# Placeholders in the job lists of a two-layer encoder: key steps one dense chunk further on, first inverse two further on in layer 2

## The chip, the core and the metric

The kernel runs on one core of a Trainium2 chip. The metric is device time in microseconds, lower is better. A matrix product runs on TensorE (PE), elementwise work on VectorE (DVE), ScalarE (ACT) and GpSimd (POOL); transfers are issued from the queues of SyncE (SP), ACT and POOL and carried by 16 DMA engines.

## The reference, cut to what matters

A trunk of two layers over 1024 tokens and 16 learned ones, width 1024, in float32. Each layer norms its input, projects it, and runs two groups side by side: a chunked gated delta rule in both directions (four heads of 128) and a gated short convolution. Their outputs go through one projection and a residual, then a SwiGLU block.

```
h = h + hybrid_mixer(rmsnorm(h), w_in, ...)       # per layer
h = h + swiglu(rmsnorm(h), w_gate_up, w_down)

# in hybrid_mixer
q, k, v = split(silu(conv3(qkv)));  q = l2norm(q);  k = l2norm(k)
# in the delta rule, per chunk, head and direction
M = strict_lower(beta * k @ k.T * decay);  A = M + I
u = solve(A, beta * v);  w = solve(A, beta * k * exp(G))
attn = q @ k.T * decay;  q_dec = q * exp(G)
# then a scan over the chunks: S, o
y_sc = sc_b * conv3(sc_c * sc_h)
out = concat(norm(o) * silu(z), y_sc) @ w_out
```

## The kernel before, in words

The sequence is worked on as nine chunks: one of 16 tokens and eight of 128. Features lie on the 128 partitions and tokens along the free axis (1040 columns).

**Dense work.** `dense` (L141 to L170) forms a product of a weight tile with eight tiles of the input, for one stretch of columns (a chunk of the dense work) at a time. Float32 exactness comes from splitting both factors into a high and a low part, so one dense chunk is 8 x 3 = 24 products (L156, L157, L158) into a bank `pacc`. A full row tile has three dense chunks, 348 or 346 columns wide; the z tiles of the last layer and some others have two, 512 wide. An eviction follows on DVE (`to_row`, L295). Weights come in as `raw` (L128, SP's queue) and are split on ACT (L129) and on POOL or DVE (L130).

**Job lists.** After each dense chunk `dense` takes one entry off each of `jobs`, `jobs2` and `jobs3` and calls it; `None` is a placeholder that lets one dense chunk go by. So the small steps of the delta rule are strewn among the large products. This fixes the order in which the program is written; the order on each engine is then decided by a scheduler, which places instructions by priority and by when its own timeline has their operands ready. `low` (L685) gives a step the priority of the dense products around it.

**Order within a layer.** Four key tiles, then four query tiles, then four value tiles, then the gated convolution and the z tiles.

- After the fourth key tile the key lengths are ready: `normalise` (L408) takes the root on ACT (L412) and the reciprocal on DVE (L413), sends them out and back as a row on all partitions by POOL's queue (L415, L418), and scales the keys head by head on DVE (L419).
- `k_out` (L421), one call a chunk: four transposes of the keys on PE (L427) into the single bank `pa`, a copy on ACT (L429) into a tile `kt`, a store by ACT's queue (L430).
- `chunk_p` (L448), one call a chunk: products of the keys with themselves (L456) into a bank `pb`; for each direction a load of decays `gd` by ACT's queue (L459), an addition on DVE (L460), the exponential on ACT (L462), a store to `dtd` by ACT's queue (L463) and the product into `P` on DVE (L465).
- `sub_start` (L511) copies the diagonal blocks of 32 x 32 on ACT (L521) and transposes them on DVE (L523). `substitute` (L525) solves these blocks by 31 steps of two instructions on DVE (L533, L535).
- `invert` (L537) builds the inverse of the 128 x 128 blocks from them in seven steps, each an entry of `jobs3`. It begins with two transposes on DVE (L544, L545) and four copies on ACT (L547). The first step multiplies on PE (L560, 128 products of 32 x 32 into `pf`, for the second direction into `pb`) and copies on ACT (L563); the second likewise (L568, L571), the third (L578, L579 to L582), the fourth (L589, L590) and the fifth (L594, L595).
- `chunk_a` (L483), one call a chunk: products of keys with queries (L489) into one of two banks `pb`; for each direction a load `eg` by ACT's queue (L493), a product on DVE (L494), a store by SP's queue (L496), a load `dt` of what `chunk_p` stored (L498, ACT's queue), a product on DVE with the bank (L499), a store by SP's queue (L501).
- `v_store` (L693), three calls a value tile: transposes on PE into `pa` (L695, L706), a copy on DVE into `vm` (L699) or on ACT (L707), a store (L702, L708).
- `z_tile` (L673) and the value tiles apply a Silu on ACT (L678, L720), the key and query tiles too (L632, followed by a square, L633, whose sums over the partitions are formed on PE, L606); `conv` (L306 to L309) is a copy on ACT and two steps on DVE.

The small tiles `eg`, `dt`, `kt`, `vm`, `rows` and a few more share one tag (`ck2`) with five buffers, used in turn. The banks of PSUM are `pacc` (three), `pa` (one), `pf` (two) and `pb` (two).

The steps of the first inverse enter `jobs3` as the fourth value tile begins (L716); those of the second inverse follow later, among the z tiles.

Of the kernel before, what the change touches and what calls it, by code (L numbers as in the profile page):

```python
# [42 lines left out]
def trunk(ctx: ExitStack, tc: tile.TileContext, xT, w_in, w_ba, w_out, w_gu, w_dn,  # L43
# [8 lines left out]
    def nm(p):  # L52
        cnt[0] += 1
        return f"{p}_{cnt[0]}"

    def big(tag, dt=F32):
        return sb.tile([128, 4, L], dt, tag=tag, name=nm(tag))
# [4 lines left out]
    def t2k(tag):  # L62
        return sb.tile([128, 4, 128], F32, tag="ck2", bufs=5, name=nm(tag))

    def c4k(tag="c"):
        return sb.tile([128, L], F32, tag="c", bufs=2, name=nm(tag))

    def bank(tag):
        return psp.tile([128, 512], F32, tag=tag, bufs={"acc": 3, "a": 1, "f": 2, "b": 2}[tag], name=nm("p" + tag))

    def pa():
        return bank("a")
# [47 lines left out]
    jobs, jobs2, jobs3 = [], [], []  # L120
# [158 lines left out]
    for l in range(DEPTH):  # L279
# [9 lines left out]
        def inproj(i, evac, pool=None, chunks=FULL):  # L289
            ws = pre.pop(i) if i in pre else wload(w_in[l, i], KT)  # L290
            dense(ws, x, chunks, evac, pool)

        def to_row(t):
            def f(ps, n0, n1):
                tt(out=t[:, n0:n1], in0=ps, in1=rstd[:, n0:n1], op=ALU.mult)  # L295
            return f

        def to_row_late(t):
            def f(ps, n0, n1):
                nc.vector.tensor_copy(t[:, n0:n1], ps)  # L300
            return f

        def trow():
            return row(Y[1], F32, 3)
# [27 lines left out]
        def gate_weights():  # L332
            dma(wr, w_ba[l])
            act(out=wb[:, :, 0:16], in_=wr, func=AF.Copy)
            tt(out=wb[:, :, 16:32], in0=wr, in1=wb[:, :, 0:16].bitcast(F32), op=ALU.subtract)
# [85 lines left out]
        def k_out(c):  # L421

            n = 16 if c == 0 else 128
            s0 = 0 if c == 0 else 16 + 128 * (c - 1)
            ps = pa()
            for h in range(H):
                nc.tensor.transpose(ps[0:n, h * 128:(h + 1) * 128], KTt[:, h, s0:s0 + n], ident)  # L427
            kt = t2k("kt")
            act(out=kt[0:n].rearrange("p a b -> p (a b)"), in_=ps[0:n], func=AF.Copy)  # L429
            adma(vkd[c, 0:n, 1, :], kt[0:n].rearrange("p a b -> p (a b)"))  # L430
# [10 lines left out]
        def span(c):  # L441
            return (16, 0) if c == 0 else (128, 16 + 128 * (c - 1))
# [3 lines left out]
        def chunk_p(c):  # L446

            if not Pd:  # L448
                Pd.extend(sb.tile([128, 4 * L], F32, tag=f"P{d}", name=nm("P")) for d in range(2))
                Pv.extend(p[:, 0:4096].rearrange("p (q i) -> p q i", i=128) for p in Pd)  # L450
                p_ = sb.tile([128, 4 * L], F32, tag=Y[0][2], name=nm("ptm"))
                ptm.extend(p_[:, 512 * i:512 * i + 512].rearrange("p (h i) -> p h i", h=4) for i in range(8))
            n, s0 = span(c)
            kk = bank("b").rearrange("p (h i) -> p h i", h=4)
            for h in range(H):
                mm(kk[0:n, h, 0:n], KTt[:, h, s0:s0 + n], KTt[:, h, s0:s0 + n], start=True, stop=True)  # L456
            for d in (dirs0 if c == 0 else (0, 1)):
                gr = ptm[(2 * c + d) % 8]
                adma(gr[0:n, :, 0:n], gd[36 * d + 4 * c:36 * d + 4 * c + 4, 0:n].partition_broadcast(n))  # L459
                tt(out=gr[0:n, :, 0:n], in0=gr[0:n, :, 0:n], in1=off[0:n, d, 0:n].unsqueeze(1).to_broadcast([n, 4, n]), op=ALU.add)  # L460
                for h in range(H):
                    act(out=gr[0:n, h, 0:n], in_=gr[0:n, h, 0:n], func=AF.Exp, scale=-1.0, bias=nGb[0:n, d, c, h:h + 1])  # L462
                adma(dtd[c, d].rearrange("p (h i) -> p h i", h=4)[0:n, :, 0:n], gr[0:n, :, 0:n])  # L463
                dst = P0[d] if c == 0 else Pv[d][:, 4 * c - 4:4 * c, :]
                tt(out=dst, in0=kk[0:n, :, 0:n], in1=gr[0:n, :, 0:n], op=ALU.mult)  # L465
                if c == 0:

                    def meta():
                        mt = t2k("mt").rearrange("p a b -> p (a b)")[0:4].rearrange("p (w a b) -> p w a b", w=2, a=16)
                        Wm, Zm = mt[:, 0], mt[:, 1]  # L470
                        Tm = t2k("mt").rearrange("p a b -> p (a b)")[0:4, 0:256].rearrange("p (a b) -> p a b", a=16)
                        dma(m0d[d, 0].rearrange("h j i -> j h i"), P0[d])
                        dma(Wm, m0d[d, 0])
                        dma(Zm, eye_d[0:4, :, :][:, 0:16, 0:16])
                        for s in (range(15, 0, -1) if d == 0 else range(0, 15)):
                            r0, r1, a0, a1 = (0, s, s, 16) if d == 0 else (s + 1, 16, 0, s + 1)
                            sh = [4, r1 - r0, a1 - a0]
                            ptt(out=Tm[:, r0:r1, a0:a1], in0=Wm[:, r0:r1, s:s + 1].to_broadcast(sh), in1=Zm[:, s:s + 1, a0:a1].to_broadcast(sh), op=ALU.mult)
                            ptt(out=Zm[:, r0:r1, a0:a1], in0=Zm[:, r0:r1, a0:a1], in1=Tm[:, r0:r1, a0:a1], op=ALU.subtract)
                        dma(m0d[d, 1], Zm)  # L480
                        dma(P0[d], m0d[d, 1].rearrange("h j i -> j h i"))

                    meta()  # L483
# [26 lines left out]
        def sub_start():  # L510

            nonlocal Tm
            tmp0.append(big(Y[0][2]))
            Tm = sb.tile([128, 2, 128], F32, tag="off", name=nm("Tm")).rearrange("p a b -> p (a b)")
            v = [tmp0[0][:, i, 0:1024] for i in range(4)]
            for d in range(2):
                W, Xi = (v[0], v[2]) if d == 0 else [c4k("x")[:, 0:1024] for _ in range(2)]
                W, Xi, dg = (t.rearrange("p (a b) -> p a b", a=32) for t in (W, Xi, v[3 - 2 * d]))
                dma(Xi, eye_d)
                for b in range(4):  # L520
                    act(out=dg[B[b]], in_=Pv[d][B[b], :, B[b]], func=AF.Copy)  # L521

                nc.vector.transpose(out=W, in_=dg.rearrange("p q i -> p i q"))  # L523
                subs[d] = W, Xi
# [106 lines left out]
        def lengths(which, q, row_, buf):  # L631
            act(out=row_, in_=row_, func=AF.Silu)  # L632
            act(out=buf, in_=row_, func=AF.Square)  # L633
            jobs.append(lambda: sums(which, q, buf))

        seq = (4, 5, 6, 7, 0, 1, 2, 3)
        for pos, i in enumerate(seq):
            hh = pos % 4
            if pos == 2:
                gate_weights()  # L640
                evp[0] = base - 60000
            lov[0] = pos > 3
            t = trow()
            late = pos < (2, 1)[l]
            inproj(i, to_row_late(t) if late else to_row(t), pfirst if l == 0 and pos == 1 else None)
            if late:
                tt(out=t, in0=t, in1=rstd, op=ALU.mult)
            dst = (QT if i < 4 else KTt)[:, hh, :]
            conv(t, dst, P_CV + 3 * i)
            if i >= 4:  # L650
                lengths("k", hh, dst, t)
            if pos == 2:
                g, negG, nGb, negE, gl, bkd = gates()
            nxt = seq[pos + 1] if pos < 7 else 8
            if nxt not in pre:
                pre[nxt] = wload(w_in[l, nxt], KT)
            if pos == 3:
                jobs.append(None)
                jobs.extend([lambda c=c: k_out(c) for c in range(9)])
                jobs2.extend([None, None] + [lambda c=c: chunk_p(c) for c in range(9)])  # L660

        for hh in range(4):
            lengths("q", hh, QT[:, hh, :], c4k("sq"))
        qs_ = jobs[-4:]
        del jobs[-4:]
        jobs.extend([None, None, None, lambda: [f() for f in qs_]])
        sub_start()
        substitute(0)

# [41 lines left out]
        for i in range(4):  # L711
            t = trow()
            if i == 2:
                jobs2.extend([lambda c=c: chunk_a(c) for c in ca])
            if i == 3:
                jobs3.extend(invert(0))  # L716
            inproj(8 + i, to_row(t))
            v = trow() if i % 2 == 0 else row(Y[1] + "f")
            conv(t, v, P_CV + 3 * (8 + i))
            act(out=v, in_=v, func=AF.Silu)  # L720
            jobs.extend([lambda i=i, v=v, c0=c0: v_store(i, v, c0) for c0 in (0, 1, 5)])
# [157 lines left out]
        for i, (d, s) in enumerate(order):  # L879
            at_prio(base - 17000 + 4000 * (1 - d) + 400 * s)  # L880
            c = s if d == 0 else 8 - s
# [108 lines left out]
        for m in range(KT + 2):  # L990
# [14 lines left out]
            else:  # L1005
                c = pcol(P_N2 + k)
# [496 lines left out]
```

## Time and profile before

| | |
|---|---|
| time, median of 3 runs | 2607.66 us (2607.26 to 2610.53) |
| the profiled execution's own time | 2614.81 us |
| its span, first to last instruction | 2612.7 us |
| mean granted TensorE clock | 0.984 |
| PE busy | 2508.1 us, 96% |
| DVE busy | 1654.4 us, 63% |
| ACT busy | 1045.9 us, 40% |
| POOL busy | 1105.0 us, 42% |
| DMA, mean rate over the span | 137 GB/s |

How to read it: times in the trace count from the first instruction of the span. Layer 1's steps named above lie at about 120 to 300 us, layer 2's at about 1418 to 1610 us. In a row of the timeline the bracket at the end gives how long the engine had been idle and what ended that. A row of the waits has the line that waited, what it waited for, the total, the number of times, and the longest. An instruction on PE is shown with its whole time in the pipeline, so the pace of a row of products is the distance of their starts.

### The profile page before, as it was taken

The page shows a single profiled execution, that of the slowest core. Times are in us where ns is not written, and L with a number is a line of the kernel's source. Part 1 is how long each engine was busy: PE and PEld are TensorE (multiplying, and loading weights), DVE is VectorE, ACT ScalarE, POOL GpSimd, SP SyncE. Part 2 cuts the span into 40 slices and gives each one's busy share as a digit, 9 for nine tenths or more (in the row PEclk, how much of TensorE's full clock was granted, in tenths as well). Part 3 has the DMA queues.
Part 4 walks back from the last instruction along what each step waited for, and adds up shares of the span by engine and source line. Part 5 has one row for each costly group of instructions (what it writes and reads, how often), then busy time and mean ns, then how long its engine had stood idle before and what let it go on. Part 6 is the DMA issues. An engine that isn't in the chain of part 4 may idle for free.

```text
span 2612.7 us, 45153 instructions
## 1 busy us (share of the span) xinstructions
PE 2508.1 (96%) x17442; PEld 2294.1 (88%) x17442; DVE 1654.4 (63%) x2481; ACT 1045.9 (40%) x1933; POOL 1105.0 (42%) x838
## 2 busy tenths in 40 slices
PE   8999999999999999989999989999989999998997
PEld 6989999898899999989999978998967778886876
DVE  4688433648766666667656874236688777668656
ACT  5664322435233333434445633324452333333444
POOL 2141311225666666645321203122367667665552
PEclk9999999999999999989999999999999999999998
DMA  3458264524422222763324581545333222248431
GB/s 126 135 185 268 90 215 148 176 80 125 135 91 99 94 74 74 252 198 111 97 86 136 186 283 63 182 159 197 116 121 129 94 102 85 79 141 273 133 108 65
DMA packets 213571, 360.03 MB, mean 138 GB/s; under 512 B 25268, under 2 KB 87676, under 8 KB 213356
## 3 DMA queue, kind: packets, MB, share of 16 engines
q1 hardware_dynamic: 180684, 310.69, 36.1%
q10 hardware_dynamic: 30496, 42.09, 5.1%
q0 software_dynamic: 2176, 4.36, 0.6%
q8 instruction: 137, 2.24, 0.4%
q14 instruction: 78, 0.64, 0.1%
HBM read 266.60 MB, written 90.46 MB: 137 GB/s over the span
## 4 chain that ended last, share of the span: by engine, by line
PE 54%; DVE 9%; DMA 4%; issue 3%; POOL 2%; ACT 1%; POOLq 0%; ACTq 0%; DVEq 0%; SPq 0%
PE pacc L156 5%; PE pacc L158 5%; PE pacc L157 5%; PE pacc L1060 3%; PE pacc L1062 3%; PE pacc L1061 3%; PE pb L1060 2%; PE pf L1060 2%; PE pb L1062 2%; PE pb L1061 2%; PE pf L1062 2%; PE pf L1061 2%; PE pacc L1400 1%; PE pacc L1402 1%; PE pacc L1401 1%
## 5 line engine op out<-in xcount | busy, mean ns | idle before, releaser
L130 POOL TENSOR_TENSOR wlo<-raw,whi 128x512 fp32r<-128x512 f32 x132 | 177.0, 1342 | 788.3 <-ACT whi L129 639.4
L156 PE MATMUL pacc<-a,whi 128*128 128x346 f32 (+1 forms) x808 | 265.5, 332 | 10.2 <-ACT whi L129 8.3
L158 PE MATMUL pacc<-a,wlo 128*128 128x346 f32 (+1 forms) x808 | 265.1, 330 | 0.4 <-DVE wlo L130 0.4
L156 PE MATMUL pacc<-b,whi 128*128 128x346 f32 (+2 forms) x672 | 234.8, 350 | 0.0
L158 PE MATMUL pacc<-b,wlo 128*128 128x346 f32 (+2 forms) x672 | 233.2, 348 | 0.0
L157 PE MATMUL pacc<-a,whi 128*128 128x346 f32 (+1 forms) x688 | 227.5, 331 | 2.7 <-DVE a L900 2.5
L129 ACT ACTIVATE whi<-raw 128x512 fp32r<-128x512 f32 x168 | 105.3, 629 | 244.6 <-PE pacc L157 169.3
L157 PE MATMUL pacc<-b,whi 128*128 128x346 f32 (+2 forms) x580 | 200.5, 347 | 0.5 <-DVE b L900 0.5
L156 PEld LDWEIGHTS pacc<-a,whi 128*128 128x128 f32 x808 | 154.5, 192 | 14.5 <-ACT whi L129 10.1
L1043 POOL TENSOR_TENSOR wlo<-rw,whi 128x512 fp32r<-128x512 f32 x92 | 134.8, 1467 | 71.7 <-ACT whi L1042 70.0
L158 PEld LDWEIGHTS pacc<-a,wlo 128*128 128x128 f32 x808 | 154.5, 191 | 2.1 <-issue 0.8
L157 PEld LDWEIGHTS pacc<-a,whi 128*128 128x128 f32 x688 | 132.2, 192 | 7.1 <-issue 2.9
L156 PEld LDWEIGHTS pacc<-b,whi 128*128 128x128 f32 x672 | 127.3, 190 | 11.0 <-issue 3.1
L158 PEld LDWEIGHTS pacc<-b,wlo 128*128 128x128 f32 x672 | 127.3, 190 | 9.2 <-issue 0.8
L1043 POOL TENSOR_TENSOR a<-rw,a 128x512 fp32r<-128x512 f32 x64 | 105.6, 1651 | 69.5 <-ACT a L1042 69.3
L1043 POOL TENSOR_TENSOR b<-rw,b 128x512 fp32r<-128x512 f32 x64 | 92.0, 1439 | 82.3 <-ACT b L1042 49.5
L157 PEld LDWEIGHTS pacc<-b,whi 128*128 128x128 f32 x580 | 109.9, 190 | 7.8 <-DVE b L900 1.0
L1042 ACT ACTIVATE whi<-rw 128x512 fp32r<-128x512 f32 x92 | 57.8, 630 | 146.5 <-DVE rw L1270 84.8
L1266 DVE TENSOR_TENSOR rw<-rw,rw 128x512 f32<-128x512 f32 x44 | 67.4, 1532 | 49.9 <-POOL wlo L1043 34.6
L1271 DVE TENSOR_TENSOR rw<-raw,rw 128x512 f32<-128x512 f32 x44 | 97.4, 2214 | 1.2
L1043 POOL TENSOR_TENSOR wlo<-raw,whi 128x512 fp32r<-128x512 f32 x50 | 76.6, 1533 | 36.5 <-ACT whi L1042 27.9
L1042 ACT ACTIVATE b<-rw 128x512 fp32r<-128x512 f32 x64 | 40.2, 630 | 119.8 <-PE pacc L1061 32.3
(970 smaller groups left out, 8420.2 us busy)
## 6 DMA issues: line engine op xcount, KB each, us to landing
raw<-in_w_in SPq DMA_DIRECT2D x112, 256.0 KB
raw<-in_w_gu SPq DMA_DIRECT2D x104, 256.0 KB
rw<-in_w_gu SPq DMA_DIRECT2D x88, 256.0 KB
rec<-aqd SPq DMA_DIRECT2D x62, 256.0 KB
rec<-vkd SPq DMA_DIRECT2D x61, 256.0 KB
rw<-in_w_dn SPq DMA_DIRECT2D x70, 192.0 KB
raw<-in_w_out SPq DMA_DIRECT2D x48, 256.0 KB
b<-ad SPq DMA_DIRECT2D x45, 260.0 KB
```

The lines of the kernel that those rows point to most:

```text
L129: act(out=hi, in_=raw[:, 0:kk, :], func=AF.Copy)
L130: (tt if lov[0] else ptt)(out=lo, in0=raw[:, 0:kk, :], in1=hi.bitcast(F32), op=ALU.subtract)
L156: mm(ps[:, :n], wh, xh[:, n0:n1], start=(k == 0), stop=False)
L157: mm(ps[:, :n], wh, xl[:, n0:n1], start=False, stop=False)
L158: mm(ps[:, :n], wl, xh[:, n0:n1], start=False, stop=(k == K - 1))
L1042: act(out=hi, in_=src, func=AF.Copy)
L1043: ptt(out=lo, in0=src, in1=hi.bitcast(F32), op=ALU.subtract)
L1060: mm(ps[:, :CW], w[0][:, k, :], th[:, cs], start=first and k == 0, stop=False, skip_group_check=True)
L1061: mm(ps[:, :CW], w[0][:, k, :], tl[:, cs], start=False, stop=False, skip_group_check=True)
L1062: mm(ps[:, :CW], w[1][:, k, :], th[:, cs], start=False, stop=stop and k == nk - 1, skip_group_check=True)
L1266: tt(out=s1t, in0=A21, in1=A22, op=ALU.add)
L1271: tt(out=A21, in0=A11, in1=A21, op=ALU.subtract)
```

## The change

Two edits in the order in which steps are put into the job lists; nothing that is computed changes.

1. After the fourth key tile, in both layers: two placeholders instead of one stand ahead of the nine `k_out` in `jobs`, and three instead of two ahead of the nine `chunk_p` in `jobs2`. An `assert` states that `jobs2` is empty before `sub_start`.
2. At the fourth value tile: `2*l` placeholders stand ahead of the steps of `invert(0)` in `jobs3`, with `l` the layer counted from 0. So there are none in layer 1 and two in layer 2.

```diff
             if pos == 3:
-                jobs.append(None)
-                jobs.extend([lambda c=c: k_out(c) for c in range(9)])
-                jobs2.extend([None, None] + [lambda c=c: chunk_p(c) for c in range(9)])
+                jobs.extend([None, None] + [lambda c=c: k_out(c) for c in range(9)])
+                jobs2.extend([None, None, None] + [lambda c=c: chunk_p(c) for c in range(9)])
...
         jobs.extend([None, None, None, lambda: [f() for f in qs_]])
+        assert not jobs2
         sub_start()
         substitute(0)
...
             if i == 3:
-                jobs3.extend(invert(0))
+                jobs3.extend([None] * (2 * l) + invert(0))
             inproj(8 + i, to_row(t))
```

## The prediction

> **What bounds the kernel now.** I read the page's busy times first.
>
> ```profile
> span 2612.7 us, 45153 instructions
> PE 2508.1 (96%) x17442; PEld 2294.1 (88%) x17442; DVE 1654.4 (63%) x2481; ACT 1045.9 (40%) x1933; POOL 1105.0 (42%) x838
> ```
>
> TensorE (PE) is busy for 96% of the span. The change adds and removes no product, so the time can only move with PE's idle time (about 2612.7 − 2508.1 = 105 us) and with the pace of its products. I read PE's waits next, and quote those beside the moved steps (line waited, total, times, longest).
>
> ```profile
> PE pf L560 <- DVE a L544: 6.0, 1, 6.0
> PE pa L427 <- DVE a L419: 3.1, 1, 3.1
> PE pa L427 <- ACT kt L429: 2.3, 2, 1.4
> PE pa L706 <- DVE vm L699: 2.1, 2, 1.7
> PE pf L560 <- DVE b L544: 0.7, 1, 0.7
> ```
>
> These five sum to 14.2 us; with 1.14 at L489 in layer 1 (quoted below) that is nearly all that the two edits can touch directly. The two largest lie in layer 2: 5.95 us where the first inverse (L560) waits for the vector transposes L544, and 3.08 us where the first key transpose (L427) waits for the scaled keys of L419. Third, PE's timeline and the windows in layer 2, which show what follows such a gap (columns of the windows: stretch, length, then busy time and count of PE, its load side, DVE, ACT, POOL, then clock, DMA share, GB/s).
>
> ```profile
> 1418.25 0.38 PE L427 MATMUL pa<-ident,a 128*16 128x128 f32 x1 [3.08 <-DVE a L419]
> 1527.65 0.39 PE L156 MATMUL pacc<-b,whi 128*128 128x512 f32 x1
> 1527.88 0.39 PE L157 MATMUL pacc<-b3f,whi 128*128 128x512 f32 x1
> 1534.92 3.62 PE L560 MATMUL pf<-a,P 32*32 32x32 f32 x128 [5.95 <-DVE a L544]
> 1538.47 1.11 PE L706 MATMUL pa<-ident,a 128*128 128x128 f32 x4
> 1539.38 1.85 PE L489 MATMUL pb<-a,a 128*128 128x128 f32 x8
> 1554.88 1.12 PE L706 MATMUL pa<-ident,a3f 128*128 128x128 f32 x4 [1.73 <-DVE vm L699]
> 1534.90:1538.40 3.50, 3.48 (x128) 3.48 (x128) 3.46 (x7) 1.68 (x2) 0.00 (x0) 0.50 0.77 238
> 1538.40:1541.40 3.00, 3.00 (x20) 2.87 (x16) 2.81 (x9) 2.95 (x4) 0.00 (x0) 0.56 0.81 259
> 1554.90:1558.00 3.10, 3.10 (x12) 3.10 (x13) 3.07 (x5) 2.48 (x4) 1.12 (x1) 0.50 0.62 209
> ```
>
> After the 5.95 us gap the granted clock is 0.50 and then 0.56 for 6.5 us. If all products went by the clock, 0.50 x 3.50 + 0.44 x 3.00 = 3.1 us are lost there. The least is what the larger products show: L489's 1.85 against 1.16 at full clock in layer 1 (quoted below), and L706's 1.11 against 0.66 for the same four transposes in the row of 144.82 below, together 1.1. I take the middle, 2.1. After the 1.73 gap, 0.50 x 3.10 = 1.55 are lost.
>
> **Why the inverse waits.** DVE's groups from 1463 to 1535 (count, busy, mean ns, idle before), then the timelines of DVE, ACT and SP:
>
> ```profile
> L494 DVE TENSOR_TENSOR eg<-a,eg 128x512 f32<-128x512 f32 x9 | 6.2, 687 | 6.8 <-DMA eg<-ged 6.8
> L499 DVE TENSOR_TENSOR dt<-pb,dt 128x512 f32<-128x512 f32 x9 | 6.1, 683 | 5.8 <-DMA dt<-dtd 5.8
> ```
>
> ```profile
> 1526.60 0.17 DVE L535 TENSOR_TENSOR a<-a,Tm 128x31 f32<-128x31 f32 x1
> 1532.36 0.69 DVE L499 TENSOR_TENSOR dt<-pb,dt 128x512 f32<-128x512 f32 x1 [5.59 <-DMA dt<-dtd]
> 1532.96 1.90 DVE L544 STREAM_TRANSPOSE a<-a 128x1024 f32<-128x1024 f32 x1
> 1538.48 0.67 DVE L499 TENSOR_TENSOR dt<-pb,dt 128x512 f32<-128x512 f32 x1
> 1521.82 0.36 ACTq L493 DMA_DIRECT2D eg<-ged  x1
> 1526.07 0.33 ACTq L498 DMA_DIRECT2D dt<-dtd  x1
> 1528.43 0.36 ACTq L498 DMA_DIRECT2D dt<-dtd  x1
> 1536.69 1.06 ACT L547 ACTIVATE P<-a 32x1024 f32<-32x1024 f32 x1 [7.26 <-DVE Tm L533]
> 1536.70 0.33 ACTq L498 DMA_DIRECT2D dt<-dtd  x1
> 1533.08 0.32 SPq L501 DMA_DIRECT2D aqd<-dt  x1
> ```
>
> The substitution (L533/L535) is done at 1526.77. L544 needs nothing else, but stands on DVE behind a product L499 that sits 5.59 us for its dt tile, whose load was issued at 1526.07 and used at 1532.36: 6.3 us. So 5.59 of the 5.95 belong to the order on DVE. eg, dt, kt and vm tiles share one ring of five buffers (load on ACT's queue, product on DVE, store on SP's queue): a buffer loaded at 1526.07 is stored at 1533.08 and loaded again at 1536.70, a turn of 10.6 us.
>
> **The change part by part.** The built order of the changed kernel's instructions shows where each step goes; a scheduler decides that, and it doesn't follow the placeholders one for one.
>
> Keys (first hunk). In layer 2 the first L427 comes ahead of five dense products that it followed before: at 1418 these are 346 or 348 wide, which at full clock go at the pace of 214.83 to 214.99 below, 0.16 us, so PE arrives 0.8 us earlier. L419 waits for the DMA of the lengths either way:
>
> ```profile
> 1416.95 1.24 DVE L419 TENSOR_TENSOR a<-a,bc 128x1040 f32<-128x1040 f32 x1 [5.38 <-DMA bc<-rnd]
> 214.83 0.32 PE L157 MATMUL pacc<-a,whi 128*128 128x348 f32 x1
> 214.99 0.32 PE L158 MATMUL pacc<-a,wlo 128*128 128x348 f32 x1
> ```
>
> The wait becomes 3.9: **0.8 us lost** (bounds 0 to 1.5). The other key steps move by under 2.4 us of PE's work; in layer 1 some stand later, which gives the single transpose bank more time to be copied out:
>
> ```profile
> 138.22 0.66 PE L427 MATMUL pa<-ident,b 128*128 128x128 f32 x4 [0.91 <-ACT kt L429]
> 144.82 0.66 PE L427 MATMUL pa<-ident,b 128*128 128x128 f32 x4 [1.36 <-ACT kt L429]
> ```
>
> From these 2.27 us at most, and nothing at least, I take **0.6 gained**.
>
> Inverse of layer 2 (second hunk). L560 does not move back on PE: it comes ahead of 26 products 512 wide that it followed, 26 x 0.23 = 6.0 us, and of some ten small ones (about 1.3), 7.3 us in all. On DVE, L544 now follows seven products L499 and six L494 instead of ten and nine, so the 5.59 us wait stands behind it. About 7.5 us of DVE's work goes behind it: six of these products at 0.68, and one L308, L130, L295 and L699. The substitution starts 0.7 us earlier, as its block copies L521 no longer stand behind a Silu on ACT. I leave the other waits for loads (the 6.8 of L494) as they are: L544 starts at 1532.96 − 5.59 − 7.5 − 0.7 = 1519.2 and ends at 1521.1. PE reached L560 at 1534.92 − 5.95 = 1528.97; now 1528.97 − 7.3 + 0.8 = 1522.5, with 1.4 us to spare. **5.95 + 2.1 = 8.05 gained there.**
>
> Next late: the eighth chunk's L489. It reuses the bank of the sixth, so it needs that chunk's second L499, which ended at 1538.48 + 0.67 = 1539.15, and PE began at 1539.38: it has no slack today. PE would reach it at about 1534.0. On ACT the four copies L547 (4 x 1.06) and the copies L563, which wait for PE, now stand ahead of loads that they followed, while the ring holds these loads to about 1526 anyway. The load issued at 1528.43 then issues at about 1529.5; 6.3 for the load and DVE's queue behind it put that L499's end near 1537.5 (1536 to 1539). **A wait of 3.5 us returns** (2 to 5), and with it a window at half clock, **1.5**. The wait at 1554.88 (1.73 + 1.55) is for a tile of the same ring; PE is then only some 3 us earlier, so I count half, **1.6 gained** (0 to 3.3). Layer 2: −0.8 + 8.05 − 3.5 − 1.5 + 1.6 = 3.85.
>
> Layer 1's inverse has no new placeholder, yet moves too: L560 comes ahead of 21 products, 3.3 us, and of L489, 4.2 us in all.
>
> ```profile
> 212.26 0.69 DVE L499 TENSOR_TENSOR dt<-pb,dt 128x512 f32<-128x512 f32 x1 [4.67 <-DMA dt<-dtd]
> 217.60 1.95 DVE L544 STREAM_TRANSPOSE b<-b 128x1024 f32<-128x1024 f32 x1
> 217.73 1.16 PE L489 MATMUL pb<-b,b 128*128 128x128 f32 x8 [1.14 <-DVE dt L499]
> 219.60 3.32 PE L560 MATMUL pf<-b,P 32*32 32x32 f32 x128 [0.71 <-DVE b L544]
> 220.00:223.50 3.50, 3.50 (x118) 0.51 0.46 149
> 223.50:227.00 3.50, 3.50 (x14) 0.51 0.54 186
> ```
>
> There the L499 with the 4.67 us wait stays ahead of L544. The substitution starts 3.4 us earlier (L521 ahead of a Silu here too), so its rest fits into that wait; L544 starts at about 212.9 and ends at 214.8. PE comes to L560 at about 213.3: a wait of 1.5 in place of 0.71 and 1.14, and the half clock of 220 to 227 stays in some place. **0.3 lost**, with −1.5 to +2 as bounds.
>
> Sum: 0.6 − 0.3 + 3.85 = **4.1 us gained**. The profiled execution took 2614.8, so 2610.7 for its like; the median of the runs shown is 2607.66, so **2603.5**.
>
> **A rule weighed.** By the rows, a gap of 1.73 us is already followed by 0.50. The Trainium skill, in "TensorE: Matmul & The Clock Gate", part 1 on the HAM clock gate, says that the clock is halved after at least one idle window of about 3.4 us. By that rule the returning wait of 3.5 would lie at the edge and one of 3 cost no clock; the sum would be up to 1.5 us better, 2602.0. The page adds that the window runs freely; that alone doesn't explain 1.73, and I keep the rows.
>
> **Rivals.**
>
> *Nothing takes the wait's place.* If the sixth chunk's last L499 ends by 1534, as PE arrives, the 5.0 stay and the wait at 1554.88 goes whole: layer 2 gives −0.8 + 8.05 + 3.3 = 10.5, with layer 1's 0.3 10.8: 2596.9. For it: DVE's seven products fewer in the inverse's way. Against it: L489 has no slack today and the ring's turn is 10.6 us.
>
> *The ring loses half a turn* (the slower one). If a load stuck behind L563 on ACT (which waits for PE, which waits for that load's bank) comes half a turn late, 5.3 us, the sixth chunk's L499 ends at 1544.4 and PE begins the eighth L489 5.3 us later than today, whatever was gained before it. The half clock of today stays, one window more follows the longer gap (1.5), nothing comes back at 1554.88, and 0.3 is gained in layer 1: 6.5 lost, 2614. For it: ACT keeps its order, and L547 with L563 take some 6.6 us of it. Against it: the loads are held by the stores to about 1526 in any case. It decides from the point where that L499 ends after 1539.15.
>
> *The change does not do what it says.* The steps named as later stand earlier in the built order, by choice of the scheduler. If what DVE waits for only changes its place (a load instead of L544, in the same us), the time stays at 2607.7, within 1.5.
>
> **How the numbers follow.** Small gain with a returning wait, 2600 to 2608: 0.42. Nothing in its place, 2594 to 2600: 0.22. Half a turn lost, 2609 to 2617: 0.26. No effect: 0.10. A measurement tells 0.2%, 5.2 us, from no change, so faster means below 2602.4 and slower above 2612.9. Faster: the second case and a third of the first, 0.36. Slower: most of the third, 0.2. The rest, 0.44. The range 2595 to 2614.5 leaves out a tenth of either end.
>
> **What would show it.** Right: no wait of L560 for L544 in layer 2, L499 with its wait behind L544; a new wait of L489 for dt of 2 to 5 us near 1534 and a clock of 0.5 behind it; 3.9 at the first L427; in layer 1 1 to 2 us at L560. Wrong: L544 still later than 1522 (another load ahead of it on DVE), a wait at L489 of over 7 us, or new waits where the chains follow (L589, L594, the second inverse).

## The result and the profile after

The changed kernel took 2618.93 us (median of 8, 2617.41 to 2627.35) against 2610.02 of before beside it: a ratio of 1.0034, interval 1.0023 to 1.0046. Measured once more later, it was 2615.91 against 2609.29: 1.0022, interval 1.0009 to 1.0035. It is 0.2 to 0.35% slower, some 6 to 9 us, where 4.1 us of gain were forecast. The trace that is shown first took 2627.35, 8.4 above its own median, so sizes are read from several executions below.

The page of the changed kernel:

```profile
span 2625.6 us, 45152 instructions
PE 2512.3 (96%) x17442; PEld 2292.3 (87%) x17442; DVE 1650.8 (63%) x2481; ACT 1046.0 (40%) x1933; POOL 1105.2 (42%) x838
```

The same products, 4.2 us more busy time on PE and 8.7 us more idle time: part of the loss is waiting, part is the pace. PE's waits in the changed kernel, for the lines that the prediction spoke of and those that came up beside them:

```profile
PE pacc L156 <- ACT whi L129: 10.4, 3, 6.8
PE pb L489 <- DVE dt L499: 9.9, 4, 6.4
PE pa L427 <- DVE a L419: 2.8, 2, 1.9
PE pb L456 <- DVE P L465: 2.1, 1, 2.1
PE pa L427 <- ACT kt L429: 1.7, 3, 1.0
PE pf L560 <- DVE a L544: 1.3, 1, 1.3
PE pf L560 <- DVE b L544: 0.9, 1, 0.9
PE pacc L156 <- DVE b L730: 0.9, 1, 0.9
```

The 5.95 us at L560 of layer 2 became 1.25. L489 went from 1.1 to 9.9 in all, 6.41 of it in one wait. Waits for L465, L129 and L730 are new or longer.

**Layer 2.** The timeline of PE, then of DVE and ACT, around the first inverse (this layer starts 7.1 us later than in the trace before):

```profile
1530.28 2.21 PE L560 MATMUL pf<-a,P 32*32 32x32 f32 x128 [1.25 <-DVE a L544]
1549.87 2.07 PE L489 MATMUL pb<-a,a 128*128 128x128 f32 x8 [6.41 <-DVE dt L499]
```

```profile
1528.23 2.00 DVE L544 STREAM_TRANSPOSE a<-a 128x1024 f32<-128x1024 f32 x1
1530.12 1.91 DVE L545 STREAM_TRANSPOSE a<-a 128x1024 f32<-128x1024 f32 x1
1533.15 0.68 DVE L494 TENSOR_TENSOR eg<-a,eg 128x512 f32<-128x512 f32 x1
1536.14 0.67 DVE L494 TENSOR_TENSOR eg<-a,eg 128x512 f32<-128x512 f32 x1
1547.77 0.69 DVE L494 TENSOR_TENSOR eg<-a,eg 128x512 f32<-128x512 f32 x1 [5.00 <-DMA vkd<-a]
1549.13 0.68 DVE L499 TENSOR_TENSOR dt<-pb,dt 128x512 f32<-128x512 f32 x1
```

```profile
1532.07 4.29 ACT L547 ACTIVATE P<-a 32x1024 f32<-32x1024 f32 x4 [2.67 <-DVE Tm L533]
1535.95 0.36 ACTq L493 DMA_DIRECT2D eg<-ged  x1
1537.42 0.33 ACTq L498 DMA_DIRECT2D dt<-dtd  x1
1541.26 0.35 ACTq L493 DMA_DIRECT2D eg<-ged  x1
1541.74 0.36 ACTq L498 DMA_DIRECT2D dt<-dtd  x1
```

L544 and L545 take DVE for 3.8 us, and the ring's next product (L494, 1533.15) stands behind them; L547 takes ACT for 4.3, and the ring's next load (1535.95) stands behind it. The dt load that the eighth L489 hangs on is issued at 1541.74; in the trace before it was issued at 1528.43, which is 1535.5 when shifted by the 7.1 us, so 6.2 us earlier. Its product L499 stands on DVE behind an L494 before which DVE was idle for 5.00 us; that one's own load was issued at 1541.26, though the row names a store. L499 ends at 1549.8, and PE starts behind it.

The windows of PE there (busy time and count, clock, DMA share, GB/s):

```profile
1545.00:1549.80 4.80, 0.00 (x0) 0.50 0.84 269
1549.80:1555.00 5.20, 5.13 (x32) 0.50 1.02 330
1555.00:1562.00 7.00, 7.00 (x61) 0.50 0.46 170
1562.00:1566.00 4.00, 4.00 (x35) 0.99 0.72 234
```

The wait is followed by 12 us at half clock with PE busy nearly all the time. If every product went by the clock, 6.1 us of pace are lost there. This is not all new: over this layer's stage, as it is marked out below, the clock records that are kept with the traces have 17.1 us at half clock here and 13.7 in the trace before.

**Layer 1.** ACT's timeline before, then after:

```profile
154.40 1.07 ACT L632 ACTIVATE b<-b 128x1040 f32<-128x1040 f32 x1
155.50 1.07 ACT L633 ACTIVATE sq<-b 128x1040 f32<-128x1040 f32 x1
156.48 8.54 ACT L521 ACTIVATE b<-P 32x1024 f32<-32x1024 f32 x8
165.67 0.63 ACT L129 ACTIVATE whi<-raw 128x512 fp32r<-128x512 f32 x1
```

```profile
156.81 8.57 ACT L521 ACTIVATE b<-P 32x1024 f32<-32x1024 f32 x8 [0.70 <-DMA dtd<-ptm]
166.02 1.28 ACT L632 ACT_TABLE_LOAD   x1
167.31 1.07 ACT L632 ACTIVATE b<-b 128x1040 f32<-128x1040 f32 x1
168.29 1.14 ACT L129 ACTIVATE whi<-raw 128x512 fp32r<-128x512 f32 x2
```

The Silu L632 with its table load moved behind the eight block copies. The weight split L129, which PE needs, stood behind the copies before; now it stands behind the copies and the Silu. PE's rows for the new waits in the trace after:

```profile
141.10 0.57 PE L456 MATMUL pb<-b 128*128 128x128 f32 x3 [2.06 <-DVE P L465]
168.96 0.43 PE L156 MATMUL pacc<-a,whi 128*128 128x348 f32 x1 [1.05 <-ACT whi L129]
219.52 2.21 PE L560 MATMUL pf<-b,P 32*32 32x32 f32 x128 [0.87 <-DVE b L544]
223.93 0.93 PE L489 MATMUL pb<-b,b 128*128 128x128 f32 x3 [2.19 <-DVE dt L499]
285.55 0.43 PE L156 MATMUL pacc<-a,whi 128*128 128x346 f32 x1 [0.86 <-DVE b L730]
```

DVE at the second inverse, before and then after. The transposes L544 stood behind both parts of the eviction L730 (348 and 346 columns wide) and now stand between them:

```profile
275.90 0.51 DVE L730 TENSOR_TENSOR b<-pacc,b 128x346 f32<-128x346 f32 x1
276.32 2.19 DVE L544 STREAM_TRANSPOSE b<-x 128x1024 f32<-128x1024 f32 x1
```

```profile
278.63 0.51 DVE L730 TENSOR_TENSOR b<-pacc,b 128x348 f32<-128x348 f32 x1
279.06 2.21 DVE L544 STREAM_TRANSPOSE b<-x 128x1024 f32<-128x1024 f32 x1
284.97 0.94 DVE L730 TENSOR_TENSOR b<-pacc,b 128x346 f32<-128x346 f32 x2
```

**How sizes are taken.** Two landmarks stand on PE ahead of all that moves and behind it: L388 once a layer (first and last start in its row) and the second inverse's first L594 (into `pb`). Before, then after (rows of one line: durations, then first and last start):

```profile
L388 PE MATMUL pb<-g,ones x4: 275/292/309, 83.6 to 1389.2; 128*128 128x72 f32 x4
L594 PE MATMUL pb<-P,b x64: 218/218/267, 315.4 to 329.4; 64*64 64x64 f32 x64
L594 PE MATMUL pb<-P,a x64: 218/218/267, 1634.8 to 1648.7; 64*64 64x64 f32 x64
```

```profile
L388 PE MATMUL pb<-g,ones x4: 275/292/309, 84.3 to 1396.3; 128*128 128x72 f32 x4
L594 PE MATMUL pb<-P,b x64: 218/218/267, 324.2 to 338.1; 64*64 64x64 f32 x64
L594 PE MATMUL pb<-P,a x64: 218/218/267, 1646.3 to 1660.2; 64*64 64x64 f32 x64
```

Layer 1's stage is 315.4 − 83.6 = 231.8 before and 324.2 − 84.3 = 239.9 after; layer 2's 1634.8 − 1389.2 = 245.6 and 1646.3 − 1396.3 = 250.0. So 8.1 and 4.4 us of the 12.9 in the span. The same subtraction for every execution (us; from unrounded starts, so 0.1 beside the rows at times):

| kernel | layer 1 | layer 2 |
|---|---|---|
| before; inverse_only | 231.9; 233.9 | 245.7; 243.0 |
| keys_layer1 | 237.7 | 242.0 |
| keys_layer2 | 233.8 | 245.0 |
| keys_layer2_inverse, and again twice | 234.1; 234.2; 231.9 | 241.7; 247.8; 246.0 |
| the changed kernel, three times | 239.8; 240.1; 240.0 | 250.0; 250.9; 248.8 |
| evict_first | 236.5 | 249.0 |
| half_copies_late | 241.0 | 238.4 |
| half_and_evict | 238.9 | 238.6 |
| loads_on_sp | 239.7 | 238.2 |
| layer2_half, twice | 232.7; 235.1 | 243.1; 239.3 |
| layer2_half_sp | 235.0 | 245.3 |
| before_l2_sp | 237.7 | 239.7 |

The ten executions with layer 1 in its old order took 231.9 to 237.7 (mean 234.0), the four with the changed kernel's order 237.7 to 240.1 (mean 239.4): 5.4 us. In layer 2 the old order took 242.0 to 245.7 (mean 243.6, three executions), the new one 241.7 to 250.9 (mean 247.5, six). Of these six, the three of the changed kernel have a mean of 249.9; the three with layer 1 in its old order have 245.2, with the same order of PE's products in layer 2.

The stages split into PE's idle and busy time and the time at half clock in the clock records (means, us, rounded):

| stage | length | idle | busy | at half clock |
|---|---|---|---|---|
| layer 1, old order (ten) | 234.0 | 8.7 | 225.3 | 4.8 |
| layer 1, new order (four) | 239.4 | 11.6 | 227.9 | 8.5 |
| layer 2, old order (three) | 243.6 | 9.1 | 234.5 | 13.7 |
| layer 2, new order (six) | 247.5 | 11.9 | 235.7 | 13.1 |

### The profile page after: what moved, and what is told of

The parts are those of the page before. It is cut to its first block, busy times and chain, and to the rows that moved or that the text cites. A ratio compares the mean times of both kernels' runs of the same rounds, so it can differ in the third digit from the quotient of the medians.

```text
span 2625.6 us, 45152 instructions
## 1 busy us (share of the span) xinstructions
PE 2512.3 (96%) x17442; PEld 2292.3 (87%) x17442; DVE 1650.8 (63%) x2481; ACT 1046.0 (40%) x1933; POOL 1105.2 (42%) x838
## 5 line engine op out<-in xcount | busy, mean ns | idle before, releaser
L156 PE MATMUL pacc<-a,whi 128*128 128x346 f32 (+1 forms) x808 | 265.3, 332 | 11.9 <-ACT whi L129 10.4
L156 PE MATMUL pacc<-b,whi 128*128 128x346 f32 (+2 forms) x672 | 235.7, 351 | 0.4 <-DVE a L730 0.4
L158 PE MATMUL pacc<-b,wlo 128*128 128x346 f32 (+2 forms) x672 | 232.7, 348 | 0.0
L129 ACT ACTIVATE whi<-raw 128x512 fp32r<-128x512 f32 x168 | 105.0, 628 | 240.4 <-PE pacc L157 174.5
L156 PEld LDWEIGHTS pacc<-a,whi 128*128 128x128 f32 x808 | 154.0, 191 | 18.1 <-ACT whi L129 11.5
L156 PEld LDWEIGHTS pacc<-b,whi 128*128 128x128 f32 x672 | 127.2, 189 | 10.8 <-issue 2.3
```

The source lines that it names most:

```text
L129: act(out=hi, in_=raw[:, 0:kk, :], func=AF.Copy)
L156: mm(ps[:, :n], wh, xh[:, n0:n1], start=(k == 0), stop=False)
L158: mm(ps[:, :n], wl, xh[:, n0:n1], start=False, stop=(k == K - 1))
```

## The experiments

The expectations measure layer 1 from the 600th to the 2100th product on PE and layer 2 from the 10200th to the 12600th; the first stage contains the first stretch, and the second stretch begins some 67 us ahead of the second stage, where nothing moves.

**Which part makes the loss.** The key placeholders in one layer alone:

```diff
-                jobs.extend([None, None] + [lambda c=c: k_out(c) for c in range(9)])
-                jobs2.extend([None, None, None] + [lambda c=c: chunk_p(c) for c in range(9)])
+                k_late = 2 - l                      # keys_layer1;  1 + l for keys_layer2
+                jobs.extend([None] * k_late + [lambda c=c: k_out(c) for c in range(9)])
+                jobs2.extend([None] * (1 + k_late) + [lambda c=c: chunk_p(c) for c in range(9)])
```

> Only the key placeholders of layer 1; layer 2 and the inverse as before. Theory A (each layer's loss comes from its own key placeholders): layer 1 loses what the two traces show between 106 us and 300 us, 8.0 us, of which the later stages give 1.6 back: 6 to 8 us slower than before, with waits of L456 for L465 (2 us), of L156 for whi (1 us), of L489 for L499 (2 us). Rival B (a spread between executions of the same program): within 2 us of before. My prediction's sum for this layer was 0.3 us gained.

Measured 2610.64 against 2607.54: 1.0010 (0.9999 to 1.0021). The stage took 237.7, 3.7 above the old mean, with waits of 1.43 at L456, 1.13 at L156 and 2.18 at L489. The waits are theory A's; the total is about half of what it expected, and its interval, from 0.3 us gained to 5.5 lost, does not exclude rival B. The stage and the repeated waits speak for a loss.

> Only the key placeholders of layer 2. In the built order this alone moves L560 ahead by 7.3 us of TensorE's work, as the whole change does. Theory A: layer 2 loses some 4 us, as the whole change's trace does from 1400 us to 1620 us, with the wait of 6 us at the eighth L489. Rival C (the loss of layer 2 comes from the inverse's placeholders, which then let a later step in ahead of that L489): no loss, 0 to 4 us faster than before, since the wait of 5.95 us is gone.

Measured 2609.15: 1.0004 (0.9994 to 1.0014). The wait at L560 fell to 1.3 and one of 4.02 came at the eighth L489. Neither theory: no loss that can be measured, and no gain.

The same with the inverse's `[None] * (2 * l)`:

> The key placeholders and the inverse's two placeholders, both in layer 2 alone; layer 1 as before. Theory A: the same as with the key placeholders of layer 2 alone, within 1.5 us. Rival C: 3 to 5 us slower than those alone. Either way about 4 us slower than before if the whole change's trace is typical, and with the run that has layer 1's placeholders alone it adds up to the whole change's 9 us.

Measured 2611.8: 1.0014 (1.0005 to 1.0023). About 4 us slower than before, as forecast either way; 2.7 us above the key placeholders of layer 2 alone, between A and C. With layer 1's 3.1 it makes 7.4, and the changed kernel measured 6.6 to 8.9. The parts add up within their intervals.

The inverse's placeholders alone:

> Only the inverse's two placeholders. The built order of all five engines is then instruction by instruction that of before, so the time should be that of before within its spread, under 2 us, and the trace shows how far the waits of one and the same order move between executions (expected: under 1 us each).

Measured 2607.31: 1.0005 (0.9994 to 1.0016), no difference. But the waits moved by far more than 1 us. PE's waits in this execution, for the same order as before:

```profile
PE pf L560 <- DVE a L544: 2.4, 1, 2.4
```

and in the execution with layer 1's placeholders alone, where layer 2 is in the old order too:

```profile
PE pf L560 <- DVE a L544: 4.0, 1, 4.0
```

So the wait of 5.95 on which the prediction rests is 2.4, 4.0 or 5.95 by the execution: DVE was idle for 1.49, 3.60 and 5.59 before the same product L499. The second hunk alone does nothing because L544, L545 and L547 are put into the program where `invert(0)` is called, ahead of its placeholders, and the later steps did not move either: the order of PE's products in this trace is that of the trace before, one for one.

**The changed kernel again.**

> The changed kernel once more, for a second trace of it. The first one's layer 2 lies 8 us above that of another execution with the same order of layer 2 (the run with both edits in layer 2 alone), with 17 us at half clock against 7. Theory A (the losses that belong to the order repeat, the long half clock does not): 2614 to 2619 us; layer 1 between 106 and 300 us again 5 us longer than in the four traces with its old order; L156 waits 1.1 for whi near 169 us and 0.9 for L730 near 285 us; the eighth L489 of layer 2 waits 4 to 6.5 us. Rival B (a spread between executions): those waits move by more than 1 us.

Measured 2615.91 against 2609.29. The waits repeat: 1.30 for whi, 0.88 for L730, 5.46 at the eighth L489, and layer 1's stage is 240.1. The long half clock of 17 us repeated too, against theory A.

**Layer 1's new waits.** The second inverse held behind the last eviction:

```diff
-            nc.vector.transpose(out=XB..., in_=Xi...)
+            after(nc.vector.transpose(out=XB..., in_=Xi...), evicted[0] if d == 1 else None)
```

with `evicted[0]` the latest L730.

> The changed kernel with the second inverse's transposes L544 held on DVE behind the last eviction L730, as they stand in the order of before; nothing else moves. Theory A: the wait of 0.9 near 285 us in layer 1 goes and with it 1.4 us of that stretch, 1.4 us faster than the changed kernel. Rival (the wait is only moved to the inverse's own products later): no gain, and a new wait at L560 or L563 of the second inverse.

Measured 2612.77: 1.0015 (1.0002 to 1.0027), 3 us under the changed kernel beside it. The wait for L730 went; PE then waited 0.40 for whi there. The stage is 236.5, 3.5 under the changed kernel's; the place itself (from the 2000th to the 2070th product) went from 12.6 to 11.8, so it gave 0.8 and not 1.4. The rest of the 3.5 is not the hold's: PE's order up to the 2038th product is the changed kernel's, and some 2.5 us of the difference stand there already.

The second half of the block copies held behind the Silu:

```diff
-                    act(out=dg[B[b]], in_=Pv[d][B[b], :, B[b]], func=AF.Copy)
+                    after(act(out=dg[B[b]], in_=Pv[d][B[b], :, B[b]], func=AF.Copy), silus[-1] if d else None)
```

with `silus` the list of the Silus L632.

> The changed kernel with the block copies L521 of the second direction held behind the fourth query tile's Silu on ACT; those of the first direction stay ahead of it. In the built order the weight split L129 then comes some 4 us earlier after the copies, and in layer 2 the first inverse and the eighth L489 stand on PE where they stood before the change. Theory A (the Silu behind eight copies costs 1.5 us in layer 1 through L129; in layer 2 the earlier inverse brings nothing): no wait of L156 for whi near 169 us, 1.5 us or more faster than the changed kernel in layer 1; in layer 2 the wait at L560 returns (2 to 6 us) and the one at the eighth L489 goes, about even. Rival (the loss of layer 1 lies in the keys themselves): under 0.5 us gained in layer 1.

Measured 2612.2: 1.0012 (0.9999 to 1.0024). The wait for whi near 169 went, as theory A has it. But layer 1 gained nothing, 241.0, which is what the rival expects; theory A can answer that another wait, the one for L730, grew:

```profile
PE pacc L156 <- DVE b L730: 3.1, 1, 3.1
```

Layer 2 took 238.4, 11.5 under the changed kernel's 249.9 and 5.2 under the old order, where "about even" was expected: the wait at L560 did not return, and L489 waited 3.2.

Both holds:

> The changed kernel with both holds, the late half of the copies and the second inverse behind the last eviction. Theory A: the wait of 3.06 for L730 that the first hold alone left at 283 us goes, layer 1 from product 600 to 2100 at 187 to 188 us against 191.7, layer 2 stays at 299 us: 3 to 5 us faster than with the first hold alone, so about the time of before or 1 to 2 us under it. Rival (that wait turns into one for another operand): no gain over the first hold alone.

Measured 2609.88: 1.0004 (0.9994 to 1.0015), the time of before and 2.3 us under the late half of the copies alone (1.3 when each is taken against its own before), less than expected. L730's wait went, and 1.68 for whi took its place at 285 us: the rival, in part. Layer 1 still took 238.9, with PE idle for 11.2 us of it.

**Layer 2's loads.** eg and dt by SP's queue:

```diff
-                    adma(eg[:, :, 0:n], ged[...])        # and the dt load alike
+                    dma(eg[:, :, 0:n], ged[...])
```

> The changed kernel with the loads of eg and dt (L493, L498) issued by SP's queue instead of ACT's. They then no longer stand behind L547 and L563 on ACT, but among SP's stores; the built order moves the first inverse of layer 2 back to within 0.7 us of its old place. Theory A (the loads stuck behind the inverse's copies on ACT made the wait at the eighth L489): that wait falls under 1 us, and layer 2 is 3 to 5 us faster than in the changed kernel. Rival (the ring of five buffers and the DMA's 6 us set the pace, whichever queue issues): the wait stays at 4 us or moves to another L489 or L560.

Measured 2609.6: 1.0003 (0.9991 to 1.0015), 6.3 us under the changed kernel beside it. The eighth L489 waited 0.99, layer 2 took 238.2, and layer 1 gained nothing (239.7). The built order moves the inverse back as well, so this doesn't tell the queue from the place. The kernel before with the same loads on SP's queue in layer 2 alone (`dma if l else adma`) does:

> The kernel before, with the loads of eg and dt in layer 2 on SP's queue; keys and inverse in their old places to within 0.8 us. Theory A (the queue matters only where the inverse's copies stand ahead of the loads on ACT): the tenth dt load was held by a store, not by ACT, so the wait at L560 stays at 2 to 6 us and the time within 2 us of before. Rival (ACT's queue delays the loads in any order): the wait at L560 goes, 4 us faster.

Measured 2606.47 against 2608.22: 0.9984 (0.9974 to 0.9994). The wait at L560 fell to 0.4, and 1.80 and 1.47 came at L489; layer 2 took 239.7. The gain is 1.8 us by the medians and 4 by the ratio. That is nearer to the rival: it points to ACT's queue holding the loads back in the old order too.

**The version that followed.** Layer 1 as before; in layer 2 both edits and the late half of the copies (`silus[-1] if d and l else None`):

> Both edits in layer 2 alone, with the second direction's block copies held behind the Silu in layer 2 alone; layer 1 in the order of before. Theory A (each layer's time goes with its own order): layer 1 as in the traces with the old order (182.6 to 184.8 us from product 600 to 2100), layer 2 as in the run with the late half of the copies (299.3 us from product 10200 to 12600, against 303 to 307 with the old order): 3 to 5 us faster than before. Rival B (what a layer takes depends on the execution, not on the order): layer 2 anywhere from 299 to 312.

Measured 2603.74 against 2608.22: 0.9983 (0.9973 to 0.9993). The total is what theory A said; layer 2 is not, 243.1 with 17 us at half clock. So it was measured again:

> The kernel that was 4.5 us faster than before, measured again: both edits and the late half of the copies in layer 2 alone. If its gain belongs to the order: 0.1 to 0.25% faster again, layer 2 at 299 to 304 us and layer 1 at 183 to 185 us. If it was chance: within 0.1% of before.

Measured 2606.08 against 2607.61: 0.9998 (0.9990 to 1.0007). A gain over before is not established.

> The same, with the loads of eg and dt in layer 2 on SP's queue. Theory A: the wait of 3 us at the eighth L489 that the late half of the copies left falls under 1 us, layer 2 at 296 to 299 us, 4 to 7 us faster than before. Rival (the ring and not the queue sets it): the same time as without it.

Measured 2607.58: 1.0001 (0.9991 to 1.0012), layer 2 at 245.3 with waits of 2.50 at L560 and 2.30 at L489: no gain over the run without it, as the rival says.

**The long half clock.** Three more executions:

> Both edits in layer 2 alone, a second execution. Theory A (the long half clock in layer 2 is chance of the window's phase): among this, the next run of the same kernel and two more of the changed kernel, 17 us and 7 us at half clock both turn up in either kernel. Theory B (it belongs to layer 1's new order, which reaches layer 2 by another way): 7 us here both times, 17 us in the changed kernel both times.

Measured 2610.29 against 2607.61: 1.0012 (1.0004 to 1.0021); 13.7 us at half clock after the wait of 5.09.

> Both edits in layer 2 alone, a third execution. Theory A: half clock of 17 us possible, layer 2 at 302 to 312 us. Theory B: 7 us, layer 2 at 302 to 304 us.

Measured 2608.97; 3.4 and 6.8 us at half clock, L489's wait 4.71.

> The changed kernel, third execution. Theory A: half clock between 1400 and 1640 us 7 to 20 us, not the same as in the first two. Theory B: 17 us again at the eighth L489, layer 2 at 310 to 312 us.

Measured 2618.48; 3.4 and 6.8 us at half clock, L489's wait 6.19. With that, the spell after L489's wait is 17, 17 and 7 us in the changed kernel and 7, 14 and 7 with the edits in layer 2 alone. So the spell differs within one order, as theory A says. That layer 1's order has no part in it is not shown: the kernel with the second inverse held back, whose order is the changed kernel's up to there, had 17 too, and with layer 1's new order these four executions took 248.8 to 250.9 in layer 2, with its old order 241.7 to 247.8. What does repeat is the wait: 5.5 to 6.4 in the changed kernel against 4.7 to 5.1.

## Why the prediction was wrong

The runs with one layer's edits alone split the miss. Layer 1 was forecast at 0.3 us gained and lost 3.1 by the medians. Layer 2 was forecast at 3.85 gained and lost 4.3 and, measured again, 2.7. So layer 2's sum failed most: its gain of 8.05 at L560 was too large, and the 3.5 and 1.5 that return at L489 were too small.

**Layer 1 was priced at 0.3 lost, 0.6 gained by its keys, and cost some 3 to 5 us.** Its placeholders alone cost 3.1 us by the medians and 3.7 in the stage; the four stages with the new order lie 5.4 above the ten with the old. The 0.3 lost has the wrong sign by its own figures, too: a wait of 1.5 in place of 0.71 and 1.14 is 0.35 gained. The prediction counted the block copies' earlier place only as a gain ("ahead of a Silu here too") and did not ask what stands behind the Silu. There stands the weight split L129, and PE waited 1.05 to 1.30 us for it near 169 us in every execution of that order and in none of the old one. DVE's order at the second inverse was not looked at: L544 went ahead of an eviction L730 that PE's bank waits for, 0.86 to 1.58, and the 70 products there took 12.6 to 13.3 us in the four executions against 11.1 to 11.2 in the ten. The wait at L489 that was to vanish came back as 2.2, while L560's 0.87 was less than the 1.5 forecast. That these single waits make up the whole 5.4 is not shown. Only 2.9 of it is idle time of PE; the rest is pace, and whether the half clock there belongs to the order stays open. Where a run took one of these waits away, it gave 0.8 us or nothing, and with both holds PE was still idle for 11.2 us. No run with the keys in their new place came back to the old mean.

**Layer 2's gain of 8.05 at L560 rested on one execution.** Nearly all of it was a DMA wait that the old order has with 2.4, 4.0 or 5.95 us, 4.1 in the mean. The wait of 1.25 that stayed belongs to the substitution, whose last L535 ended at 1528.2 as L544 began. That leaves 2.9 us gained by the mean. Nor did the 2.1 for the clock come: the stage had 13.7 us at half clock in each of the three executions of the old order and 6.8 to 20.5 in the six of the new, 13.1 in the mean. A wait of this size in one trace bounds what can be gained and is not itself the gain.

**The returning wait at the eighth L489 was right in place, and in cause as far as the rows show it, and too small.** Forecast 3.5 (2 to 5); measured 4.0 to 6.4 in the eight executions in which the inverse stands early in layer 2 with loads on ACT's queue. The forecast let the dt load issue 1.1 us later; in the first trace it issued 6.2 us later. There L544 and L545 hold DVE and L547 holds ACT ahead of the ring's next product and load. That this makes the load late is read from the order of the rows; no run isolates it, since the holds and the other queue moved the inverse back as well. The rival with half a ring turn (5.3) named ACT's copies and nearly this delay, though it was given 0.26. That its total, 2614, comes closer is partly luck: it had layer 2 at 6.8 lost and layer 1 at 0.3 gained. Forecast beside it and right: the wait at 1554.88 for vm is gone in the changed kernel.

**The half clock behind that wait** was priced at 1.5, one window. It was 7 to 17 us long, so at most 3.4 to 8.5 us of pace. The wait in the first trace began at 1543.46 and the half clock at 1545.00. PE had been busy for 1.68 of the 3.41 us before that, at the full clock:

```profile
1541.59:1545.00 3.41, 1.68 (x69) 1.00 0.75 238
```

The prediction weighed the rule of the Trainium skill, "TensorE: Matmul & The Clock Gate", part 1, that one idle window of about 3.4 us halves the clock. The wait is longer than that, but the clock fell 1.5 us into it, so the trace does not bear the rule out. The page has the full clock back after one busy window; 12 us of a busy PE at 0.50 in the windows above don't agree with that.

**The first key wait** was to grow from 3.08 to 3.9. It was 1.90 and another 0.94 behind it, and 0.4 to 2.6 in other executions of the new order; 3.08, 3.38, 1.62 and 1.20 in the old. So the lengths' DMA, taken as fixed, moves this wait by 2.2 us within the old order of the keys, more than the 0.8 for PE's earlier arrival.

Right was that the steps stand earlier than their placeholders say, and that layer 2's L544 goes ahead of the dt wait. The forecast failed by sizes of one sign: layer 1 near zero, L560's wait at its largest, L489's at 3.5 with one window.

## What to carry to other kernels

Where an order changes, go down each engine's new order and name, for every step that moved ahead, what now stands behind it and who waits for that; a gain at the step itself is half of the account. Read the size of a DMA wait from several executions of one order before removing it. A step that is put ahead in a loop of few buffers can cost the loop its time on every engine that it uses, and the wait shows up later at another line, as at the eighth L489 here.

## What the runs showed of the hardware

The half clock comes in spells that are multiples of 3.413 us, and within one execution all of them start on one grid: 142.12, 224.04 and 241.11 in the changed kernel's clock records are 24 and 5 steps of 3.413 apart. From execution to execution the grid lies elsewhere. The Trainium skill, in "TensorE: Matmul & The Clock Gate", part 1, says that the window is 3413 ns and runs freely; the records agree. One and the same order, with waits of 4.7 to 5.1 us at the same product, had 7, 14 and 7 us at half clock; that the grid's place makes this difference is not shown. Half a window of idle PE could be enough to start a spell, as in the row of 1541.59 above. In the two long spells of the changed kernel PE was busy with dense products and with L578's of 32 x 32; what kept the clock low there stays open.
